# Layer 1's output projection: sums made by accumulating DMAs to DRAM, the last head's y taken from SBUF, and constants that fill a multiple of 64 bytes

## The chip, the cores and the metric

The kernel runs on one core of a Trainium2 chip. The metric is the device time of one execution in microseconds; the figure for a kernel is the median over runs. Beside it stands one profiled execution, with a trace of every instruction on the core's engines: PE (TensorE; PEld is its weight load), DVE (VectorE), ACT (ScalarE), POOL (GpSimd), and SP (SyncE, which here only issues loads).

## The reference

Two layers over 1,024 latent tokens and 256 context tokens, 1,024 channels. Layer 0 has 16 neighbourhood-attention heads and 4 bidirectional mLSTM heads; layer 1 has 16 bidirectional HGRN2 heads (gated linear attention). Each layer normalises its input, projects it, runs the heads, multiplies by a SiLU gate and projects back; the result goes through a learned gate and is added to the layer's input. The end of layer 1 is what the change is about:

```python
def merge(o, z):
    o = _rms(jnp.swapaxes(o, 1, 2).astype(z.dtype), h_norm.reshape(HG_HEADS, HG_VDIM))
    return (o.reshape(o.shape[:2] + (HG_VW,)) * jax.nn.silu(z)) @ w_out
...
x = x + gate * y_lat
```

Here y is 1,024 tokens by 2,048 (16 heads of 128), w_out is 2,048 by 1,024, and only latent tokens are returned. All of it is float32.

## The kernel before

**Exact products from pairs.** A float32 operand is split into a rounded high part and a low rest (`split`, L71: an ACT copy makes the high part, a DVE subtraction the rest). A product is three matmuls per slice of 128 (high x high, high x low, low x high: `dense`, L129 to L131, and `out_sum`, L858 to L860). So every operand costs one ACT and one DVE operation per 128x512 piece before PE may use it.

**Layer 1's heads.** For each of 16 heads, `hg_proj` projects forget gates and queries, `hg_intra` climbs seven levels (L1021 and L1051; a chain of small operations over PE, ACT and DVE), `hg_vz` projects values and gates (tiles wz), `hg_ctx` and `hg_scan` carry the state along. At the end of a head POOL scales y by its norm, and `hg_out` (L1150) transposes it in two halves of 512 tokens; ACT copies each half into the one buffer gyt (L1157) and POOL stores it in DRAM (`yd2`, L1158). While heads run, POOL also makes sums of blocks of w_out (`wo_sums`) and, for the first eight heads, the difference of y's two token halves (`y_diff`, stored in `sy`).

**Layer 1's output projection.** It is a product of 2x2 blocks in Winograd's form: y is cut into two halves of tokens and two of heads, w_out into four blocks of 1,024 x 512, and seven products of sums of blocks take the place of eight. Each product has four token tiles of 128, each tile 8 slices x 3 matmuls of 512 columns. The order is: first product (y's first tokens and heads; kept in `p`), seventh (`sy` with a sum of weights; added to `u`), second (first tokens, heads 8 to 15), then fifth, sixth, third and fourth. The first two and part of the second stand in the code as work that can fill PE while head 15 runs its chains. For the fifth, sixth and third the sums of y blocks are made as they are loaded: `sums` (L1426) loads one or two 128x512 tiles over SP and adds or subtracts on DVE (L1438) into `ysum` (tile oys). The sinks f2, f5, f6, f3 (from L1451 on) move results between `p`, `u` and `e`, with adds on POOL, and `final` (L1415) loads the residual tile from the scratch `x1`, adds, multiplies by the gate, adds the residual on POOL or DVE, and stores to the output from POOL's queue (L1423). Weights come over SP into a ring of raw buffers (woraw, 4) and are split into rings on the left (wo1) or the right side of SBUF (oy, w1).

**Order.** Instructions are put in each engine's order at build time by a planner that simulates a timeline from priorities; `urgent` moves work forward, `behind` puts one instruction behind another on its engine. On the chip each engine then runs its list in order and waits on semaphores. Loads go through SP's queue, stores and the sums' loads through POOL's.

**Places in SBUF.** Pools grow from the left and from the right; every tile starts at a multiple of 32 bytes. At the left stand the constants (from `ident` on), which take 1,632 bytes per partition from an address that is a multiple of 64, and behind them the left-hand pools of both layers. On the right stand the normalised input (hh, hl), layer 1's projection weights (w1), and the output projection's pool oy; they start at multiples of 64.

## Time and profile before

| | |
|---|---|
| median of 3 runs | 3446.57 us (3445.27 to 3448.31) |
| the profiled execution's own time | 3444.31 us |
| its span in the trace | 3442.5 us |
| PE busy | 3368.1 us, 98% of the span |
| DVE busy | 2051.4 us, 60% |
| ACT busy | 1407.0 us, 41% |
| POOL busy | 664.0 us, 19% |
| moved by DMA | 333.56 MB |
| mean granted PE clock | 0.992 |

Busy time is what the trace shows an engine at work. Matmuls overlap in it: one of 512 columns shows 0.39 us though the next starts 0.23 us later, so the pace is read from starts. A kernel whose PE is busy for 98% of the time can gain in two ways: at places where PE waits (here mostly at the start and in the last 220 us), or through matmuls that follow each other faster. A wait that is not on the way to the last instruction costs nothing.

### The profile page before, as it was taken

The numbers are of one execution on the slowest core, as the hardware profiler recorded it, in microseconds if no ns is written. First come the engines' busy times: TensorE is split into PE (matmuls) and PEld (weight loads), VectorE is DVE, ScalarE is ACT, GpSimd is POOL, SyncE is SP. The second block draws the span as 40 slices with busy tenths as digits, with TensorE's granted clock in tenths as the row PEclk, the third lists the DMA queues.
The fourth block names the chain that finished last, engine by engine and source line by source line (L and its number), as shares of the span: only waits on it lengthen the run. The fifth ranks groups of instructions, "written<-read, shape, count | busy, mean of one in ns | idle before, by whom it ended". The sixth has DMA issues, their size and how long they took to land.

```text
span 3442.5 us, 64358 instructions
## 1 busy us (share of the span) xinstructions
PE 3368.1 (98%) x25044; PEld 2972.1 (86%) x25044; DVE 2051.4 (60%) x4786; ACT 1407.0 (41%) x3310; POOL 664.0 (19%) x1036
## 2 busy tenths in 40 slices
PE   7999999999999999999999999999999999999988
PEld 5689999888989888898888999989999988889866
DVE  5336666566655466777666555555555555555657
ACT  5235544455444444454354333333333333333432
POOL 2121222122211111221100111111111111121023
PEclk9999999999999999999999999999999999999999
DMA  6522222232233443444652111111111111111364
GB/s 242 214 75 70 79 77 74 76 90 83 68 90 99 144 125 121 127 132 144 218 166 71 50 58 55 58 59 58 57 59 59 50 50 50 54 59 37 119 204 151
DMA packets 327152, 333.56 MB, mean 97 GB/s; under 512 B 30696, under 2 KB 277672, under 8 KB 324800
## 3 DMA queue, kind: packets, MB, share of 16 engines
q1 hardware_dynamic: 287808, 222.76, 21.8%
q0 software_dynamic: 39040, 106.69, 8.8%
q8 instruction: 197, 3.23, 0.4%
q14 instruction: 107, 0.88, 0.1%
HBM read 259.40 MB, written 69.79 MB: 96 GB/s over the span
## 4 chain that ended last, share of the span: by engine, by line
PE 87%; DMA 4%; issue 3%; DVE 3%; ACT 1%; POOL 1%; SPq 0%; POOLq 0%; DVEq 0%; ACTq 0%
PE mm L129 19%; PE mm L131 19%; PE mm L130 19%; PE s L1021 4%; PE acc L798 2%; PE tr L778 2%; PE mm L858 2%; PE mm L859 2%; PE mm L860 2%; PE s L579 2%; PE acc L570 2%; PE acc L560 1%; PE acc L1097 1%; PE tr L1033 1%; PE acc L1098 1%
## 5 line engine op out<-in xcount | busy, mean ns | idle before, releaser
L131 PE MATMUL mm<-hh,wl 128*128 128x512 f32 (+1 forms) x1600 | 584.2, 365 | 0.0
L129 PE MATMUL mm<-hh,wh 128*128 128x512 f32 (+1 forms) x1600 | 584.1, 365 | 0.0
L130 PE MATMUL mm<-hl,wh 128*128 128x512 f32 (+1 forms) x1600 | 583.6, 365 | 0.0
L129 PE MATMUL mm<-wh,hh 128*128 128x256 f32 (+1 forms) x1520 | 473.6, 312 | 1.7 <-ACT ev L314 1.0
L131 PE MATMUL mm<-wh,hl 128*128 128x256 f32 (+1 forms) x1520 | 470.1, 310 | 0.3 <-DVE hl L273 0.3
L130 PE MATMUL mm<-wl,hh 128*128 128x256 f32 (+1 forms) x1520 | 470.3, 309 | 0.0
L131 PEld LDWEIGHTS mm<-hh,wl 128*128 128x128 f32 x1600 | 301.6, 189 | 46.0 <-issue 0.3
L129 PEld LDWEIGHTS mm<-hh,wh 128*128 128x128 f32 x1600 | 301.9, 189 | 45.3 <-issue 0.8
L130 PEld LDWEIGHTS mm<-hl,wh 128*128 128x128 f32 x1600 | 301.8, 189 | 43.4 <-issue 0.2
L129 PEld LDWEIGHTS mm<-wh,hh 128*128 128x128 f32 x1520 | 286.3, 188 | 22.7 <-ACT ev L295 4.2
L131 PEld LDWEIGHTS mm<-wh,hl 128*128 128x128 f32 x1520 | 286.2, 188 | 13.5 <-issue 1.4
L130 PEld LDWEIGHTS mm<-wl,hh 128*128 128x128 f32 x1520 | 286.8, 189 | 12.5 <-issue 1.2
L129 PE MATMUL mm<-wzh,hh 128*128 128x256 f32 x1024 | 296.1, 289 | 0.6 <-ACT gEc L945 0.6
L131 PE MATMUL mm<-wzh,hl 128*128 128x256 f32 x1024 | 291.3, 284 | 0.0
L130 PE MATMUL mm<-wzl,hh 128*128 128x256 f32 x1024 | 290.5, 284 | 0.0
L74 DVE TENSOR_TENSOR wl<-wraw,wh 128x512 fp32r<-128x512 f32 x240 | 167.0, 700 | 175.4 <-ACT wh L73 172.1
L73 ACT CAST wh<-wraw 128x512 fp32r<-128x512 f32 x240 | 147.5, 619 | 243.4 <-PE mm L130 166.2
L129 PEld LDWEIGHTS mm<-wzh,hh 128*128 128x128 f32 x1024 | 193.5, 189 | 2.9 <-ACT gEc L945 0.8
L130 PEld LDWEIGHTS mm<-wzl,hh 128*128 128x128 f32 x1024 | 193.4, 189 | 1.7
L131 PEld LDWEIGHTS mm<-wzh,hl 128*128 128x128 f32 x1024 | 193.2, 189 | 1.2
L858 PE MATMUL mm<-woh,yh 128*128 128x512 f32 x422 | 169.8, 403 | 17.8 <-DVE og L1387 10.1
L1051 ACT COPY gksel<-gK 128x1024 f32<-128x1024 f32 x96 | 111.2, 1158 | 174.4 <-PE s L1021 128.9
(382 smaller groups left out, 7359.4 us busy)
## 6 DMA issues: line engine op xcount, KB each, us to landing
wraw<-in_wab_dram SPq DMA_DIRECT2D x112, 256.0 KB
wraw<-in_wc_dram SPq DMA_DIRECT2D x96, 256.0 KB
wraw<-yd SPq DMA_DIRECT2D x94, 256.0 KB
wraw<-in_wc_dram SPq DMA_DIRECT2D x128, 128.0 KB
md<-ev POOLq DMA_DIRECT2D x60, 256.0 KB, 2.7
mloz<-md SPq DMA_DIRECT2D x40, 256.0 KB
adar<-in_wada_dram SPq DMA_DIRECT2D x8, 1024.0 KB
adar<-in_wada_dram POOLq DMA_DIRECT2D x8, 1024.0 KB, 8.8
```

The costliest lines, as they stand in the source:

```text
L73: nc.scalar.copy(hi, x)
L74: nc.vector.tensor_tensor(out=lo, in0=x, in1=hi.bitcast(F32), op=ALU.subtract)
L129: mm(ps, lhsT=lh(k), rhs=rh(k), start=(start and k == 0), stop=False)
L130: mm(ps, lhsT=lh(k), rhs=rl(k), start=False, stop=False)
L131: m = mm(ps, lhsT=ll(k), rhs=rh(k), start=False, stop=(stop and k == nk - 1))
L570: nc.tensor.matmul(num, lhsT=qc[:, j, :], rhs=C[d][:, j, :], start=False, stop=(j == 1))
L579: nc.tensor.matmul(u, lhsT=st["k"][c][:, j * P : (j + 1) * P], rhs=vw, start=True, stop=True)
L778: nc.tensor.transpose(pt[:nk, i, :], pr[:, o : o + nk], self.ident)
L798: m = nc.tensor.matmul(yp[h64], lhsT=v[:, h64], rhs=pTs[hd][:nk, i, :], start=(i == turn[0]), stop=(i == turn[-1]), tile_position=(0, hd * ...
L858: mm(ps, lhsT=yh[k], rhs=w.h(kk), start=(kk == 0), stop=False)
L1021: self.nc.tensor.matmul(out[s], lhsT=lhsT, rhs=rhs, start=True, stop=True, tile_position=(0, b * 64))
L1051: nc.scalar.copy(ksel.rearrange("p (b s i) -> p b s i", s=2, i=h), pick(K))
```

## The change

- `y_diff` now stores second half less first half (the sign is turned) into three scratch arrays, `sy`, `s3` and `s6`, not into one.
- `hg_out` also stores the second half of heads 0 to 7 into `s5`. For heads 8 to 15 it adds to those arrays with accumulating DMAs: the first half (now negated) to `s3`, the second half to `s5`, `s6` and `s3`. So the y sums for the fifth, sixth and third products lie ready in DRAM, and `sums` is gone.
- The last head's first half is split from the SBUF copy (`near`, tiles lasth and lastl) and used for the second product's last slice, for all four token tiles; the second product's other seven slices run ahead of it. Two tiles of the fifth product's first four slices run ahead too, for which two more result banks are opened.
- Layer 0 stores its latent result straight into the output tensor; at the end `final` no longer loads a residual: it accumulates gate x sum into the output by DMA. The remaining adds of `p`, `u` and `e` go from POOL to DVE, and signs are turned to match.
- The first product's first y tiles are split into a free tile of the heads, its first four weight pieces into a ring that is free earlier, and later y splits are put behind the last head's level 5 (`late`). The raw ring of weights has 3 buffers, not 4; the y raw ring of that pool has 2, not 3.
- Constants: `hnc` holds its negative too (128 bytes, not 64), and `qknp` is a column of `qkn`.

```diff
     def y_diff(self, h, pool):
...
-        nc.gpsimd.tensor_tensor(out=x, in0=x, in1=z, op=ALU.subtract)
-        nc.gpsimd.dma_start(out=self.sy[h], in_=x)
+        nc.gpsimd.tensor_tensor(out=x, in0=z, in1=x, op=ALU.subtract)
+        for dst in (self.sy, self.s3, self.s6):
+            nc.gpsimd.dma_start(out=dst[h], in_=x)
...
-    def hg_out(self, h, yn, pool, y):
+    def hg_out(self, h, yn, pool, y, near=None):
...
-            yt = self.t(pool, [P, 512], F32, "gyt", 1)
-            nc.scalar.activation(yt, pt.rearrange("p a b -> p (a b)"), AF.Copy, scale=self.hnc[:, h : h + 1])
+            yt = self.t(*((near[2], [P, 512], F32, "lasty", 1) if near else (pool, [P, 512], F32, "gyt", 1)))
+            sign = 1 if h >= 8 and c == 0 else 0
+            nc.scalar.activation(yt, pt.rearrange("p a b -> p (a b)"), AF.Copy, scale=self.hnc[:, sign, h : h + 1])
             nc.gpsimd.dma_start(out=y[h, :, c * P : (c + 4) * P], in_=yt)
+            if h < 8 and c:
+                nc.gpsimd.dma_start(out=self.s5[h], in_=yt)
+            if h >= 8:
+                for dst in (self.s5, self.s6, self.s3) if c else (self.s3,):
+                    nc.gpsimd.dma_start(out=dst[h - 8], in_=yt, accum_op=ALU.add)
+            if near and c == 0:
+                self.split(near[0], near[1], yt)
...
-            self.hnc = load("hnc", [P, 16])
-            qkn = load("qkn", [P, 2])
-            self.qkn = self.t(cp, [P, 1], F32, "qknp")
+            self.hnc = self.t(cp, [P, 2, 16], F32, "hnc")
+            nc.gpsimd.dma_start(out=self.hnc[:, 0, :], in_=a["hnc"])
...
+            qkn = self.t(cp, [P, 3], F32, "qkn")
+            nc.gpsimd.dma_start(out=qkn[:, 0:2], in_=a["qkn"])
+            self.qkn = qkn[:, 2:3]
...
-                w = block(W[0:D, 0:512], wo * 8, None, [self.rawp, 3, "wraw"])
-                self.out_part(w, 0, 0, y2, yp, lambda t, ps: nc.scalar.copy(acc[0][:, t, :], ps))
-                w = block(self.sw[1], wr * 4 + wo * 4)
-                self.out_part(w, 0, 0, S, yp, lambda t, ps: add(u[:, t, :], ps, p[:, t, :]))
-                w2 = block(W[D : 2 * D, 0:512], wo * 4 + wr * 4)
...
+                w = block(W[0:D, 0:512], wr * 4 + wo * 4, None, [pool, 3, "wraw"])
+                ps = self.ps("mm", [P, 512])
+                self.out_sum(ps, w, 0, (0,), None, yp, 2, {0: ys})
+                nc.scalar.copy(p[:, 0, :], ps)
+                self.out_part(w, 0, 0, y2, yp, lambda t, ps: nc.scalar.copy(p[:, t, :], ps), None, range(1, 4), late=self.level)
+                w = block(self.sw[1], wo * 4 + wr * 4)
+                self.out_part(w, 0, 0, S, yp, lambda t, ps: add(u[:, t, :], p[:, t, :], ps, ALU.subtract))
+                w2 = block(W[D : 2 * D, 0:512], wo * 8)
+                m2 = []
+                for t in range(4):
+                    if t == 2:
+                        banks.close()
+                        es.enter_context(self.pp.phase(c=4))
+                    m2.append(self.ps("c" if t > 1 else "mm", [P, 512]))
+                    hi, lo = self.out_y(t, 1, y2, yp, 4, ks=((0, 4), (4, 3)))
+                    self.dense(m2[t], lambda i: hi[i], lambda i: lo[i], w2.h, w2.l, 7, True, False)
...
-                def final(tt, b, x, y, eng=nc.vector):
+                def final(tt, b, x, y, op_=ALU.add):
                     r, c = slice(tt * P, (tt + 1) * P), slice(b * 512, (b + 1) * 512)
-                    xt = self.t(op, [P, 512], F32, "oxh", 3)
-                    dma(out=xt, in_=self.x1[r, c])
-                    g = self.t(op, [P, 512], F32, "og", 2)
-                    add(g, x, y)
-                    nc.vector.tensor_tensor(out=g, in0=g, in1=gates[b], op=ALU.mult)
-                    add(xt, xt, g, eng)
-                    nc.gpsimd.dma_start(out=a["out"][r, c], in_=xt)
+                    g = self.t(op, [P, 512], F32, "og", 4)
+                    add(g, x, y, op_)
+                    add(g, g, gates[b], ALU.mult)
+                    nc.gpsimd.dma_start(out=a["out"][r, c], in_=g, accum_op=ALU.add)
...
                 def f5(t, ps):
                     nc.scalar.copy(e[:, t, :], ps)
-                    add(p[:, t, :], p[:, t, :], e[:, t, :], nc.gpsimd)
-                    add(e[:, t, :], u[:, t, :], e[:, t, :], nc.gpsimd)
+                    add(p[:, t, :], ps, p[:, t, :])
                     loads()
 
                 def f6(t, ps):
-                    s6 = self.t(op, [P, 512], F32, "os", 2)
-                    nc.scalar.copy(s6, ps)
-                    final(4 + t, 1, ps, e[:, t, :], nc.gpsimd)
-                    add(p[:, t, :], s6, p[:, t, :], nc.gpsimd)
-                    add(u[:, t, :], s6, u[:, t, :], nc.gpsimd)
+                    add(u[:, t, :], ps, u[:, t, :])
+                    add(p[:, t, :], ps, p[:, t, :])
+                    final(4 + t, 1, u[:, t, :], e[:, t, :])
                     loads()
...
-                self.out_part(w5, 0, 0, sums((0, 4), (8, 4, ALU.add, False)), yp, f5)
-                self.out_part(w6, 0, 0, sums(None, (0, 0, ALU.subtract, False)), yp, f6)
-                self.out_part(w3, 0, 0, sums(None, (8, 0, ALU.subtract, True)), yp, f3)
+                m5 += [self.ps("mm", [P, 512]) for _ in range(2)]
+                for t in range(2, 4):
+                    m5_part(t, 0, raws)
+                for t in range(4):
+                    m5_part(t, 4, raws)
+                    f5(t, m5[t])
+                self.out_part(w6, 0, 0, self.s6, yp, f6, raws)
+                self.out_part(w3, 0, 0, self.s3, yp, f3, raws)
                 self.out_part(w4, 4, 1, y2, yp, lambda t, ps: final(4 + t, 0, ps, u[:, t, :]), raws)
```

More of the change, by code (lines that the diff above doesn't have):

```diff
@@ L101, in piece @@
                 c = s.shape[1]
[L102 removed]
+                self.last_dma = nc.sync.dma_start(
                     out=r3[:, :, off : off + c],
@@ L1368, in build @@
                         st = self.hg_proj(h + 1, pool)
-                    self.hg_out(h, hv["A"], pool, self.yd2)
+                    if h == 15:
+                        rh.close()
+                        yp = es.enter_context(tc.tile_pool(name="oy", bufs=1, side="right"))
+                        last = [self.t(yp, [P, 512], F32R, t, 1) for t in ("lasth", "lastl")] + [yp]
+                    self.hg_out(h, hv["A"], pool, self.yd2, last)
                     for i in [h] if h < 12 else [2 * h - 12, 2 * h - 11] if h < 14 else []:
@@ L1373, in build @@
                         self.y_diff(h - 1, pool)
[L1375 to L1377 removed]
+                self.yraws = 2
+                wo, wr, raw = [(yp, "wo", 8)], [(self.wp, "w", 4)], [yp, 3, "woraw"]
                 assert self.slabs == 4
@@ new lines, in build @@
+                ys = ([], [])
+                for i, k in enumerate((0, 4)):
+                    raw8 = self.t(pool, [P, 512], F32, "wraw", 3)
+                    dma(
+                        out=raw8.rearrange("p (j t) -> p j t", j=4),
+                        in_=y2[k : k + 4, :, 0:P].rearrange("j p t -> p j t"),
+                    )
+                    self.split(near[:, 2 * i, :], near[:, 2 * i + 1, :], raw8)
+                    for part, n in zip(ys, (2 * i, 2 * i + 1)):
+                        part += [near[:, n, j * P : (j + 1) * P] for j in range(4)]
```

128 lines of the change are left out of this document (66 added, 62 removed).

## The prediction

> **What bounds the kernel now.** I read the table of windows over the end of the kernel first, because the output projection is where the diff works. Columns: stretch, its length, then busy time and count of PE, PEld, DVE, ACT and POOL, the granted clock, the DMA share and GB/s.
>
> ```profile
> core 0: us, PE busy (x) PEld busy (x) DVE busy (x) ACT busy (x) POOL busy (x), PEclk, DMA share, GB/s
> 3222.00:3250.00 28.00, 23.02 (x214) 18.02 (x213) 23.53 (x37) 17.23 (x30) 0.00 (x0) 0.88 0.65 208
> 3250.00:3299.20 49.20, 49.20 (x262) 41.59 (x260) 23.48 (x45) 18.68 (x41) 3.10 (x4) 1.00 0.38 118
> 3299.20:3313.00 13.80, 8.12 (x29) 5.93 (x28) 5.60 (x9) 6.12 (x16) 2.88 (x4) 0.88 0.44 134
> 3313.00:3391.00 78.00, 65.12 (x249) 49.73 (x250) 66.93 (x81) 29.56 (x53) 36.33 (x29) 0.90 0.82 248
> 3391.00:3434.70 43.70, 43.66 (x184) 34.68 (x182) 28.36 (x42) 11.43 (x19) 14.52 (x15) 0.98 0.50 165
> 3434.70:3442.50 7.80, 0.00 (x0) 0.00 (x0) 2.07 (x3) 0.00 (x0) 0.54 (x1) 0.65 0.09 34
> ```
>
> PE is busy throughout the second and the fifth stretch. In the first, third and fourth it is idle for 5.0, 5.7 and 12.9 us, and what it does run there goes at a granted clock of 0.88, 0.88 and 0.90, which costs about another 2.8 (0.12 x 23), 1.0 and 6.5 us. So the tail loses 7.8 + 6.7 + 19.4 = 33.9 us to waiting. The same table in thirds of the fourth stretch, and the waits (total, times, longest), say for what:
>
> ```profile
> 3313.00:3340.00 27.00, 25.24 (x100) 19.84 (x101) 21.05 (x31) 10.44 (x19) 8.83 (x9) 0.94 1.04 311
> 3340.00:3365.00 25.00, 22.12 (x85) 16.57 (x85) 19.88 (x25) 10.78 (x20) 13.46 (x10) 0.93 0.96 292
> 3365.00:3391.00 26.00, 17.76 (x66) 13.32 (x66) 26.00 (x27) 8.35 (x15) 14.05 (x12) 0.84 0.46 141
> ```
>
> ```profile
> PE mm L858 <- DVE og L1387: 10.1, 3, 7.0
> ...
> ACT woh L73 <- DMA woraw<-sw: 23.4, 8, 9.2
> ACT yh L73 <- DVE oys L1438: 21.0, 12, 4.5
> ...
> PE mm L858 <- ACT yh L73: 3.5, 2, 1.9
> ```
>
> The first two thirds are bound by DMA (share 1.04 and 0.96; ACT waits 23.4 us for weights), the last by DVE, which is busy for all 26.00 us. The last wait row is from the first stretch: the first product lacks its split y while head 15 climbs its levels.
>
> Outside the tail PE is the bound without a gap, so there only the pace of its matmuls counts. That pace is not one number. Timeline rows (start, duration, engine, line), first and last of runs without a break:
>
> ```profile
> 1656.12 0.39 PE L858 MATMUL mm<-woh,yh 128*128 128x512 f32 x1
> ...
> 1686.11 0.39 PE L858 MATMUL mm<-woh,yh 128*128 128x512 f32 x1
> ```
>
> ```profile
> 3404.16 0.40 PE L860 MATMUL mm<-woh,yl 128*128 128x512 f32 x1
> ...
> 3434.27 0.39 PE L860 MATMUL mm<-woh,yl 128*128 128x512 f32 x1
> ```
>
> ```profile
> 191.34 0.40 PE L129 MATMUL mm<-hh,wh 128*128 128x512 f32 x1
> ...
> 201.89 0.40 PE L129 MATMUL mm<-hh,wh 128*128 128x512 f32 x1
> ```
>
> ```profile
> 1656.00:1686.00 30.00, 30.00 (x134) 1.00 0.98 303
> 3404.00:3434.00 30.00, 30.00 (x130) 1.00 0.44 140
> ```
>
> Between the starts lie 132, 129 and 45 matmuls: 227.2, 233.4 and 234.4 ns each. The two windows (PE busy and count, clock, DMA) show it by count, 134 against 130 in 30 us, both at clock 1.00. The first two runs are the same kind of matmul on the same kind of tile. What differs is where the operands lie: in the first run both are in the right-hand pool, in the others the moving one and the stationary one are on different sides. The program places every tile on a multiple of 32 bytes. The constants before it take 1,632 bytes, so every left-hand pool of weights starts 32 past a multiple of 64; the right-hand tiles start on multiples of 64.
>
> **The change part by part.**
>
> *Constants.* hnc grows from 64 to 128 bytes, and qkn takes in qknp (32 less): 1,632 becomes 1,664 = 26 x 64, and everything on the left moves by 32 bytes. Left against right then agrees modulo 64, as in the 227.2 ns run. The counts (group rows: count | busy us, mean ns; one of three lines each, the other two have the same count; first three from before 1654 us, the fourth from 3313 us on, the last from 1860 to 3222):
>
> ```profile
> L129 PE MATMUL mm<-hh,wh 128*128 128x512 f32 x384 | 152.6, 397 | 0.0
> ...
> L129 PE MATMUL mm<-wh,hh 128*128 128x512 f32 x240 | 100.3, 419 | 0.2 <-ACT wh L73 0.2
> ...
> L129 PE MATMUL mm<-wxh,hh 128*128 128x512 f32 x80 | 32.6, 410 | 0.5 <-ACT wxh L73 0.5
> ```
>
> ```profile
> L858 PE MATMUL mm<-woh,yh 128*128 128x512 f32 x136 | 56.6, 416 | 12.5 <-DVE og L1387 10.1 <-ACT yh L73 2.2
> ```
>
> ```profile
> L130 PE MATMUL mm<-wzl,hh 128*128 128x256 f32 x1018 | 288.8, 284 | 0.0
> ```
>
> Of the 136 some 128 read the left-hand ring (four products x 4 tiles x 8). 3 x (384 + 240 + 80 + 128) = 2,496 matmuls x 6.3 ns = 15.7 us; I take 15 saved, since gaps too small to see may swallow some. For 256 columns it is less clear:
>
> ```profile
> 1984.16 0.28 PE L130 MATMUL mm<-wzl,hh 128*128 128x256 f32 x1
> ...
> 1987.55 0.28 PE L129 MATMUL mm<-wzh,hh 128*128 128x256 f32 x1
> ```
>
> ```profile
> 2428.76 0.28 PE L129 MATMUL mm<-hh,wh 128*128 128x256 f32 x1
> ...
> 2431.26 0.28 PE L129 MATMUL mm<-hh,wh 128*128 128x256 f32 x1
> ```
>
> The first run (29 matmuls, 116.9 ns) has its operands on different sides, the second (21, 119.0 ns) on the same side: here agreement is slower by 2.1 ns. The wz matmuls number 3 x 1018 and some, so 6.4 us are to be lost if they go to 119.0, nothing if not. I take 4. The other 256-column products, in layer 0, I take as unchanged.
>
> By the Trainium skill (TensorE: Matmul & The Clock Gate, Part 2: What happens when you issue a matmul), PE reads weights and moving data through two independent ports, so that loading weights takes nothing from the running matmul. By that rule the shift does nothing and this term is 0, not -11; the two runs of 227.2 and 233.4 ns speak against it, unless something other than the addresses sets them apart.
>
> *The sums leave DVE and POOL.* These are group rows of DVE from 3313 to 3434.7, and the last from 3250 to 3299, where POOL is nearly idle (3.10 us):
>
> ```profile
> L74 DVE TENSOR_TENSOR wol<-woraw,woh 128x512 fp32r<-128x512 f32 x32 | 27.2, 874 | 4.4 <-ACT woh L73 4.4
> ...
> L1438 DVE TENSOR_TENSOR oys<-oys,oyz 128x512 f32<-128x512 f32 x16 | 13.8, 874 | 3.9 <-DMA oyz<-yd 2.4 <-DMA yraw<-yd 1.3
> ...
> L1438 DVE TENSOR_TENSOR oys<-oyz,oys 128x512 f32<-128x512 f32 x8 | 11.0, 1390 | 0.0
> ...
> L1387 DVE TENSOR_TENSOR oxh<-oxh,og 128x512 f32<-128x512 f32 x3 | 2.1, 692 | 0.1
> ```
>
> ```profile
> L74 DVE TENSOR_TENSOR wol<-woraw,woh 128x512 fp32r<-128x512 f32 x8 | 5.3, 690 | 2.5 <-ACT woh L73 2.5
> ```
>
> DVE loses the y sums (24.8 us) and the residual's adds (2.1), gains 12 adds from POOL (12 x 0.69 = 8.3), and its 32 weight splits go from 874 back to 690 ns without POOL beside them (-5.9). 66.93 + 28.36 = 95.3 us becomes 71 over about 100 us of matmuls: no longer the bound. Loads: of the 40 y tiles, 16 residual tiles and 32 weight pieces of the last four products, 256 KB each, the fifth product's 8 second operands and the 16 residual tiles are no longer loaded; the accumulating stores add a read each, but on the other queue. So both bounds give way. What is late next is the sixth product, whose sink has four DVE operations per tile: with two y splits and two weight splits 8 x 0.69 = 5.5 us, against 24 matmuls x 0.2272 = 5.45 us. I take 14 of the 19.4 us (bounds 6, if the weight ring, now 3 raw buffers instead of 4, keeps ACT waiting, and 19).
>
> *The last head's y from SBUF.* The second product runs seven of eight slices without head 15, then the fifth product's first four for two tiles: 84 + 24 matmuls against 24 before, 19 us more, that may run before head 15's result is there. That covers the 6.7 us of the third stretch: I take 5 (0 to 6.7). In the first stretch four weight pieces and the first y are split early into tiles that are already free: 3 of 7.8 us (0 to 6); the split copies queued behind level 5 keep ACT free for the chain.
>
> *In the heads.* Heads 0 to 7 issue three more stores, heads 8 to 15 four accumulating ones, 0.62 us of POOL each (row below). POOL idles before most of them. The place that can hurt is the single yt buffer: ACT's second copy waits until the first half's DMAs, now with an accumulation on s3, have read it. Head 11's wait has room:
>
> ```profile
> 2935.44 0.69 ACT L1157 ACTIVATE gyt<-tr,hnc 128x512 f32<-128x512 f32 x1 [4.87 <-PE tr L1155]
> ...
> 2944.49 0.69 ACT L1157 ACTIVATE gyt<-tr,hnc 128x512 f32<-128x512 f32 x1 [1.90 <-PE tr L1155]
> ```
>
> ```profile
> 2936.42 0.61 POOL L1158 DMA_DIRECT2D yd<-gyt  x1 [3.33 <-ACT gyt L1157]
> ...
> DMA to landing us min/median/max: 2.4/2.4/4.2
> ```
>
> The accumulation is issued by 2937.7 and has 6.8 us until ACT wants the buffer. The trace has no accumulating DMA. Its nearest row is the plain store, 2.4 us; a read and a write one after the other would be 4.8. Either fits. ACT's queue behind it holds the copy of v and the next level's ksel, for which PE would wait. I take 2 us over all heads (0 to 10).
>
> *The end.* After the last matmul one of the residual's adds goes (0.69, the oxh row above), and the last store becomes an accumulation: between 2.4 and 4.8 us instead of 2.4, I take +1.2. Sum +0.5 (-0.7 to +2).
>
> **Sum.** -15 + 4 - 14 - 5 - 3 + 2 + 0.5 = -30.5 us on the profiled execution's own 3444.3: 3413.8. The median of the runs is 2.3 us above that execution: 3416.
>
> **The rivals.** (a) *The addresses do nothing*: the 6 ns have another cause. For it: one agreeing pair runs slower at 256 columns. Against: two different places at 233 to 234 ns. Without -15 and +4: 3427. This is where the rule of the Trainium skill above would lead. (b) *The tail finds a new bound*: three raw buffers and the order on SP's queue keep weights late, or the sixth product holds DVE. For it: 23.4 us of waits for weights. Against: 24 of 88 loads fewer. Only 6 + 2 + 1 of the 22 us come: 3429. (a) and (b) together: 3440. (c) *Accumulations are slow*, and the kernel gets slower. Place: ACT waiting at L1157 in heads 8 to 15, PE behind it. With a landing of L us each of eight heads loses L - 8.8 (6.8 of room, some 2 us that PE's two result banks cover), and the last store L - 2.4. This eats 32 us when 8(L - 8.8) + L - 2.4 = 32, at L = 11.6, about five plain stores; at 13 us it is 3416 + 44 - 2 = 3458. For it: nothing like it was measured, and two accumulations on s3 in one head must follow one another. By the Trainium skill (DMA: Bandwidth & Descriptors, Rules for kernel authors) an accumulation must wait for the earlier one's semaphore; the trace has none to show it. Against: one read more doesn't make five stores. (d) *Better*: all of the bounds come, 19 + 6.7 + 6 in the tail, 16 and no loss from the addresses: 3446.6 - 47 = 3399.
>
> **How the numbers follow.** Forecast 3416 (its own range 3406 to 3424): 0.45. (a) 0.13, (b) 0.16, both 0.04, (c) 0.10, (d) 0.12. Range 3398 to 3440: beyond it lie (c) and the edges of (d) and of both. This kernel's times tell apart about 0.2%, 6.9 us, so faster is below 3439.7: 0.45 + 0.13 + 0.16 + 0.12, less edges, 0.83; same 0.07; slower 0.10.
>
> **What would show it.** The 3313 to 3391 stretch with DMA share under 0.9, DVE under 80% and no wait for oys; 227 ns between 512-column matmuls at 191 us; wz at 119 ns; landing of s3 under 6.8 us; PE idle in the tail under 12 us in all. It is wrong if layer 0 ends at the same time as before, if ACT's wait at L1157 grows in heads 8 to 15, or if PE waits for weights in place of sums.

## The result and the profile after

| | before | changed |
|---|---|---|
| median, us (5 runs of each, side by side) | 3445.27 (3442.29 to 3448.31) | 3416.5 (3411.4 to 3420.42) |
| ratio | | 0.9917, 95% interval 0.9906 to 0.9929 |
| profiled execution: own time / span, us | 3444.31 / 3442.5 | 3411.4 / 3409.6 |
| mean granted clock | 0.992 | 0.994 |

The kernel is faster by 28.8 us at the medians, and the prediction was 3416. The profiled execution of the changed kernel lies at the low end of its five runs: between the two traces lie 32.9 us.

The windows of the changed kernel over the end of the program (stretch, length, busy time and count of PE, PEld, DVE, ACT, POOL, then clock, DMA share, GB/s):

```profile
core 0: us, PE busy (x) PEld busy (x) DVE busy (x) ACT busy (x) POOL busy (x), PEclk, DMA share, GB/s
3218.00:3246.00 28.00, 26.88 (x232) 22.03 (x233) 20.64 (x31) 16.03 (x29) 0.00 (x0) 1.00 0.53 161
3246.00:3290.80 44.80, 44.63 (x245) 38.09 (x243) 27.30 (x52) 21.03 (x45) 2.26 (x3) 1.00 0.58 176
3290.80:3320.20 29.40, 24.33 (x108) 19.47 (x107) 13.11 (x21) 9.65 (x23) 10.50 (x13) 1.00 0.72 179
3320.20:3399.10 78.90, 78.84 (x336) 63.87 (x336) 52.77 (x85) 30.91 (x53) 9.39 (x11) 0.98 0.78 194
3399.10:3409.60 10.50, 0.00 (x0) 0.00 (x0) 1.36 (x2) 0.00 (x0) 0.85 (x1) 0.66 0.17 25
```

From 3320 on (the second half of the fifth product, then the sixth, third and fourth) PE now runs without a gap: it is idle for 0.06 us until 3399. DVE is busy for 67% of that time, where it had been busy for all of the last third before, and DMA for 78%, where it had been at 104% and 96% in the first two thirds. The first stretch has lost its idle time too (28.00 - 26.88 = 1.1 us against 5.0), and its clock is 1.00 instead of 0.88. What is left stands in the third stretch, 5.1 us, and in the fifth, where no matmul runs for 10.5 us; before, that end was 7.8.

To see where the 32.9 us come from, one follows the same piece of work through both traces. Rows of the changed kernel: the first matmul of the long run in layer 0's output (before: 1656.12), a copy of head 11's y (before: 2935.44), and the copy of the last half of the last head's y.

```profile
1651.31 0.39 PE L861 MATMUL mm<-woh,yh 128*128 128x512 f32 x1
```

```profile
2931.67 0.69 ACT L1164 ACTIVATE gyt<-tr,hnc 128x512 f32<-128x512 f32 x1 [4.85 <-PE tr L1161]
...
3301.18 0.69 ACT L1164 ACTIVATE lasty<-tr,hnc 128x512 f32<-128x512 f32 x1 [1.63 <-PE tr L1161]
```

The last of them in the kernel before:

```profile
3308.92 0.69 ACT L1157 ACTIVATE gyt<-tr,hnc 128x512 f32<-128x512 f32 x1
```

| from ... to | before, us | changed, us | gain, us | the prediction's terms there |
|---|---|---|---|---|
| start, layer 0's output | 1656.12 | 1651.31 | 4.8 | 13 (constants) |
| to head 11 | 1279.32 | 1280.36 | -1.0 | -4 (wz), -2 (heads) |
| to the last head's y | 373.48 | 369.51 | 4.0 | 3 (first stretch) |
| to the end of the last matmul | 125.74 | 97.86 | 27.9 | 5 + 14 + 2 (constants) |
| to the end of the span | 7.84 | 10.56 | -2.7 | -0.5 |

The last matmul ends at 3434.66 before and at 3399.04 after. The sum of the forecast came out right, and its terms did not: layer 0 gave a third of what it was to give, the tail gave a third more, and the end took five times its price.

Each row compares two single traces. Six kernels that are alike up to head 11 (the changed one and runs 6, 7, 9, 10 and 11) reach the place in layer 0's output between 1650 and 1655 us and head 11's copy between 2930 and 2936. So the gains of the first two rows hold only to some 3 us either way; the 27.9 of the tail is far outside such scatter.

### The profile page after: what moved, and what is told of

Same layout as the page of the kernel before. It is cut to its first block, busy times and chain, and to the rows that moved or that the text cites. A ratio compares the mean times of both kernels' runs of the same rounds, so it can differ in the third digit from the quotient of the medians.

```text
span 3409.6 us, 64360 instructions
## 1 busy us (share of the span) xinstructions
PE 3353.0 (98%) x25044; PEld 2967.1 (87%) x25044; DVE 2019.0 (59%) x4772; ACT 1401.5 (41%) x3307; POOL 666.3 (20%) x1064
## 4 chain that ended last, share of the span: by engine, by line
PE 88%; issue 4%; DMA 3%; DVE 2%; POOL 1%; ACT 1%; SPq 0%; POOLq 0%; DVEq 0%; ACTq 0%
PE mm L130 19%; PE mm L132 19%; PE mm L131 19%; PE s L1024 4%; PE acc L799 2%; PE tr L779 2%; PE mm L861 2%; PE mm L863 2%; PE mm L862 2%; PE acc L571 2%; PE s L580 2%; PE acc L561 1%; PE acc L1102 1%; PE tr L1036 1%; PE acc L1103 1%
## 5 line engine op out<-in xcount | busy, mean ns | idle before, releaser
L1071 DVE TENSOR_TENSOR gQ<-gQ,gF 128x1024 f32<-128x1024 f32 x112 | 139.2, 1243 | 54.1 <-PE s L1024 53.4
```

Source lines behind the costliest of these rows:

```text
L1071: nc.vector.tensor_tensor(out=v, in0=v, in1=tot, op=ALU.mult)
```

## The experiments

Every kernel ran on one chip with runs of the kernel before beside it, and every ratio below is to those runs, as the 0.9917 is. A difference in us between two kernels is taken from their ratios where nothing else is said, since the medians of the kernel before go from 3443.7 to 3445.6 us there. Differences of about 5 us between two such kernels are at the edge of what the runs tell apart, so where one stage is meant, the time between two events of the same trace is given too.

### 1 and 2: 32 bytes in each kernel

```diff
+            nc.vector.memset(self.t(cp, [P, 8], F32, "pad"), 0.0)
             edge = es.enter_context(tc.tile_pool(name="edge", bufs=1, side="right"))
```

> The kernel before with 32 unused bytes put behind the constants, nothing else: every left-hand tile moves by 32 bytes, as the change moves it. Theory A (from the paces in the trace of the changed kernel: matmuls of 512 columns cost 227 to 228 ns where the two operands lie a multiple of 256 bytes apart, 229 at 64 bytes from one, 232.5 at 128, 233.5 at 32 or 96; wz products get 0.8 ns slower, the other left-against-right products of 256 columns 0.9 ns faster): -1.6 -1.1 -1.7 +2.5 -3.0 -0.9 = about -6 us, 3439.5 against 3445.3 for the kernel before, ratio 0.998. The prediction's step (all 2,496 matmuls go to 227.2 ns, wz to 119.0): -11 us, ratio 0.997. Rival (a), the addresses do nothing: ratio 1.000.

> The changed kernel with 32 unused bytes behind the constants: the left-hand tiles go back to 32 past a multiple of 64, the rest of the change stays. Theory A: +6 us on the changed kernel's 3416.5, so 3422.5, ratio to the kernel before 0.9933. The prediction's step: +11, 3427.5, ratio 0.9948. Rival (a): 3416.5, 0.9917. In the trace the matmuls of layer 0 with 512 columns go from 232.5 back to 233.5-234 ns, those of the tail that take the left-hand ring from 229 to 233 ns.

Measured: the kernel before with the padding 3437.99 us, ratio 0.9981 (0.9972 to 0.9989, 11 runs), 6.5 us faster; the changed kernel with it 3424.04, ratio 0.9933 (0.9921 to 0.9946), 5.5 us slower than without. The addresses are worth about 6 us, both ways round. The expectation of 11 lies outside the first interval (9.6 at most), and 0 lies outside it too. The second run by itself settles less, since its interval overlaps that of the changed kernel.

### 3: 128 bytes more

The same line with 32 elements in place of 8, in the changed kernel.

> The changed kernel with 128 unused bytes behind the constants. Agreement modulo 64 stays as it is; the distance between left-hand and right-hand operands changes by 128 modulo 256: in layer 0 from 128 to 0. Theory A (the distance modulo 256 sets the pace): 2,112 matmuls of 512 columns in layer 0 go from 232.5 to about 227.5 ns, -10; wz products (distance 64 to the other side) between 0 and -7; layer 0's products of 256 columns +2: in all -8 to -15, 3401 to 3408, ratio 0.987 to 0.989. Rival (only modulo 64 counts, as the prediction had it): 3416.5, ratio 0.9917, and 232.5 ns stays.

Measured: 3403.72 us, ratio 0.9875 (0.9861 to 0.9888). Another 14.5 us faster than the changed kernel (12.8 at the medians), for 128 bytes that nothing uses. Rows of the timeline, first and last matmul of an unbroken run of 46 in layer 0, at the same place of the program as the run at 191 us in the prediction; changed kernel first, then the one with the padding:

```profile
189.89 0.39 PE L130 MATMUL mm<-hh,wh 128*128 128x512 f32 x1
...
200.39 0.39 PE L130 MATMUL mm<-hh,wh 128*128 128x512 f32 x1
```

```profile
191.07 0.40 PE L130 MATMUL mm<-hh,wh 128*128 128x512 f32 x1
...
201.29 0.39 PE L130 MATMUL mm<-hh,wh 128*128 128x512 f32 x1
```

45 intervals: 233.3 ns, hardly less than the 234.4 of before, and then 227.2 ns. So agreement modulo 64 was not the condition. The tail moves the other way in the same kernel; its last 321 to 326 intervals, changed kernel, then with 128 bytes:

```profile
3324.00 0.41 PE L130 MATMUL c<-woh,yh 128*128 128x512 f32 x1
...
3398.65 0.39 PE L863 MATMUL mm<-woh,yl 128*128 128x512 f32 x1
```

```profile
3316.65 0.41 PE L132 MATMUL c<-woh,yl 128*128 128x512 f32 x1
...
3391.55 0.40 PE L863 MATMUL mm<-woh,yl 128*128 128x512 f32 x1
```

229.0 ns over 326 intervals against 233.4 over 321. Windows of 74 us inside these two runs say that it isn't the clock, which is 1.00 in both:

```profile
3324.00:3398.00 74.00, 74.00 (x325) 60.64 (x324) 49.51 (x79) 28.59 (x49) 9.39 (x11) 1.00 0.77 192
```

```profile
3317.00:3391.00 74.00, 74.00 (x319) 59.63 (x318) 48.96 (x78) 28.16 (x48) 9.39 (x11) 1.00 0.76 179
```

Theory A holds. Taking each matmul's two tile addresses from the built program and the mean time to the next matmul of the same kind from the trace, one gets this (distance: address of the moving minus that of the stationary operand, modulo 256; all operands are 4 bytes an element):

```
columns  operands, place    before      changed     +32 bytes   +128 bytes
512      h,w   layer 0     160: 234.0   128: 232.6   96: 233.4    0: 228.4
512      wo,y  tail         32: 232.0    64: 228.8   96: 231.7  192: 231.8
256      wz,h  heads        32: 116.8    64: 117.6   96: 119.8  192: 114.7
256      w,h   layer 0      96: 119.6   128: 118.8  160: 118.2    0: 119.5
512      h,w   heads         0: 228.9     0: 228.5    0: 228.2    0: 228.0
```

The last row is the control: both operands lie on the same side there, so no padding moves them against each other, and it stays within 0.9 ns. With 512 columns a distance of 0 is the fastest; with 256 it is among the slowest, and 192 the fastest. That 0 and 128 differ rules out a period of 64 or 128 bytes; whether the period is 256 or a multiple of it was not tried apart.

### 4: distances chosen from that table

```diff
+            off = right.enter_context(tc.tile_pool(name="off", bufs=1, side="right"))
+            nc.vector.memset(self.t(off, [P, 16], F32, "off"), 0.0)
             self.open_h(right)
...
             lk = self.fp = l1.enter_context(tc.tile_pool(name="hgk", bufs=1))
+            nc.vector.memset(self.t(lk, [P, 32], F32, "off1"), 0.0)
...
+                nc.vector.memset(self.t(op, [P, 48], F32, "off2", 1), 0.0)
                 wl1 = wl.enter_context(tc.tile_pool(name="wo1", bufs=1))
```

> The changed kernel with three paddings and nothing else: 64 unused bytes under layer 0's right-hand operands, 128 under the left-hand tiles of layer 1's heads, 192 under the left-hand tiles of the tail. Theory A (the distance moving minus stationary operand, modulo 256, sets the pace, with the paces of the runs above: 256 columns 114.65 ns at 192, 117.6 at 64, 118.8 at 128; 512 columns 229 at 64, 231.8 at 192, 232.6 at 128, 227.2 at 0): layer 0's moving weights go from distance 128 to 192 (3,300 matmuls of 256 columns, -13.7 us; 960 of 512 columns, -0.6), its moving hh from 128 to 64 (1,152 x 3.6 = -4.1), wz from 64 to 192 (-9), the tail from 64 to 0 (-0.9): -28 us, 3388 (3384 to 3394), ratio 0.984. Rival (256 columns at 192 are fast only for wz, by its kind and not its place): -14 us, 3402, ratio 0.988.

Measured: 3394.49 us, ratio 0.9858 (0.9843 to 0.9873): the fastest of all, 22 us below the changed kernel at the medians (20 by the ratios) and 51 (49) below the kernel before. It lies between the theory (3388) and the rival (3402), and the paces say that the rival is wrong: layer 0's products of 256 columns, no wz among them, went from 118.8 to 115.5 ns in the mean. The longest unbroken run of them, first and last row, in the changed kernel and then here:

```profile
1121.53 0.27 PE L130 MATMUL mm<-wh,hh 128*128 128x256 f32 x1
...
1132.56 0.28 PE L130 MATMUL mm<-wh,hh 128*128 128x256 f32 x1
```

```profile
1109.48 0.28 PE L130 MATMUL mm<-wh,hh 128*128 128x256 f32 x1
...
1120.03 0.28 PE L130 MATMUL mm<-wh,hh 128*128 128x256 f32 x1
```

93 intervals: 118.6 and 113.4 ns. In the tail the distance is 0 now, and the pace is a little under the 228 that the table has for it, 321 intervals of 226.7 ns:

```profile
3307.40 0.40 PE L132 MATMUL c<-woh,yl 128*128 128x512 f32 x1
...
3380.17 0.39 PE L863 MATMUL mm<-woh,yl 128*128 128x512 f32 x1
```

Most of the 6 us that are missing of the 28 lie in layer 0: its moving weights of 256 columns stayed at 115.5 in the mean, not 114.65, and those of 512 got no faster (233.2 ns at 192 against 232.5).

### 5 to 7: the sums, the residual, POOL's additions, one at a time

Run 5 gives SP and DVE the sums for s6 and s3 again, in the tail; run 6 loads the residual and adds it on DVE; run 7 puts 12 additions back on POOL (the first diff below doesn't show the loader of the sums and what the heads no longer store, the last one not the four additions of the fifth product):

```diff
...
-                self.out_part(w6, 0, 0, self.s6, yp, f6, raws)
-                self.out_part(w3, 0, 0, self.s3, yp, f3, raws)
+                self.out_part(w6, 0, 0, sums(True, 0, ALU.subtract), yp, f6)
+                self.out_part(w3, 0, 0, sums(False, 8, ALU.add), yp, f3)
```

```diff
...
+                    xt = self.t(op, [P, 512], F32, "oxh", 3)
+                    dma(out=xt, in_=a["out"][r, c])
...
-                    nc.gpsimd.dma_start(out=a["out"][r, c], in_=g, accum_op=ALU.add)
+                    add(xt, xt, g)
+                    nc.gpsimd.dma_start(out=a["out"][r, c], in_=xt)
```

```diff
...
-                    add(u[:, t, :], ps, u[:, t, :])
-                    add(p[:, t, :], ps, p[:, t, :])
+                    s6 = self.t(op, [P, 512], F32, "os", 2)
+                    nc.scalar.copy(s6, ps)
+                    nc.gpsimd.tensor_tensor(out=u[:, t, :], in0=s6, in1=u[:, t, :], op=ALU.add)
+                    nc.gpsimd.tensor_tensor(out=p[:, t, :], in0=s6, in1=p[:, t, :], op=ALU.add)
```

> The changed kernel, but the y sums of the sixth and the third-weight product (s6, s3) are made in the tail again: SP loads both operands, DVE adds (16 additions), and the heads issue no accumulations onto s3 and s6 and no copies to them. s5 stays as it is. The count of 256 KB loads in the last four products is then the old one. Theory (DVE bound per product): in the sixth product each tile has 10 DVE operations of 0.69 us, 6.9 us against 5.45 us of matmuls, so 4 x 1.45 = +6 us there, less 0 to 2 us saved in the heads: 3420 (3418 to 3424), with DVE over 80% busy between 3320 and 3400. Rival 1 (DVE has room, 52.8 of 78.9 us, and only the adds on POOL had slowed it): 3416.5. Rival 2 (accumulations in the heads cost something there): the heads end over 2 us earlier.

> The changed kernel, but the residual is loaded by SP into SBUF, added by DVE and the tile stored plainly, as before the change (16 loads of 256 KB more, 16 DVE operations of 0.69 us more, no accumulations into out). Theory: 11 us more on DVE still fit (64 of 79 us), and the end after the last matmul falls from 10.6 to about 8 us: -1 (-3 to +2), 3415.5. The prediction's step (both bounds come back in part): +3 to +5 in the tail.

> The changed kernel with the additions of the sinks of the fifth and sixth product back on POOL (12 additions; ACT copies the sixth product out of PSUM for them again). Theory: POOL beside DVE takes DVE's 32 weight splits from 690 back towards 870 ns, but DVE loses the 12 additions (8.3 us): 0 to +2, 3417.5. Rival (the adds on POOL were what held the tail): over +4, 3421.

Measured: 3416.94, 3416.63 and 3417.24 us, ratios 0.9920 (0.9906 to 0.9934), 0.9921 (0.9907 to 0.9935) and 0.9922 (0.9909 to 0.9936): none can be told from the changed kernel by the time. In the traces the way from the last head's y to the end of the last matmul is 103.5, 102.5 and 102.3 us instead of 97.9, so each costs 4 to 6 us there, by one trace of each; in six kernels whose tail differs from the changed one in nothing but distances or the last store (the changed kernel and runs 2, 3, 4, 10 and 11) it lies between 97.8 and 100.6. By that measure the sums come out as expected, the residual as the prediction's step had it and not as the theory (-1) did, and POOL's additions at the theory's upper end or its rival's lower (2 to 4). The times are too close to decide any of the three.

The three do not cost at the same place. PE's longest wait behind the last head's y that the changed kernel doesn't have, in runs 5 and 6:

```profile
PE mm L861 <- DVE oacc L1412: 3.4, 1, 3.4
PE mm L130 <- ACT yh L73: 6.1, 1, 6.1
```

With the sums back, PE waits for a late addition of DVE's in a sink. With the residual back, PE waits for DVE no longer than 0.9 us; the 6.1 us are a wait at 3317.8 for ACT's split of the fifth product's y. ACT had waited there 8.3 us at a time for a weight piece, on a queue of SP's that now carries the residual tiles too; in the changed kernel its longest such wait there is 1.4 us, and PE's gap of 3.5 us at 3320 does not come on top in run 6. In run 7 PE has two waits of 1.4 and 1.1 us for splits of ACT's, and DVE's weight splits are slower:

```profile
L74 DVE TENSOR_TENSOR wol<-woraw,woh 128x512 fp32r<-128x512 f32 x22 | 16.6, 773 | 9.0 <-ACT woh L73 8.9
```

POOL is busy there for 26.6 us of 83. In run 5, with the sums on DVE but POOL at 9 us, the same 22 splits take 688 ns as in the changed kernel: it is POOL's work beside them, not DVE's load, that lengthens them.

### 8: all three together

The three diffs above in one kernel. What is left of the change in the tail is s5, the order of the products and the last head's y from SBUF.

> The changed kernel with the three edits of the runs above put back together: s6 and s3 summed in the tail, the residual loaded and added by DVE, the 12 additions on POOL. What stays of the change in the tail is the last head's y from SBUF, the order of the second and fifth product, and s5. Alone each of the three cost 0 to 1 us. Theory (each bound had room for one of them, not for all; together DVE gets 16 x 0.69 + 16 x 0.69 = 22 us more, slower beside POOL, and DMA 6 MB more): DVE is over 90% busy in the last 80 us and PE waits, +10 to +18 us, 3430. Rival (the gain of the tail is all in the order of the products and the last head's y, the sums are worth nothing): 3416 to 3419.

Measured: 3420.1 us, ratio 0.9928 (0.9916 to 0.9941): 4 us slower by the runs, which is between rival and theory; the two intervals overlap, so the runs leave room for some 10 us and for none. The trace is clearer: the way to the last matmul is 109.8 us instead of 97.9, 11.9 more. The window of the same products as above (from the fifth's second half on):

```profile
3321.10:3410.30 89.20, 82.83 (x334) 65.58 (x334) 71.29 (x100) 32.41 (x56) 29.45 (x24) 0.94 0.68 218
```

Its groups of DVE there, instructions | busy us, mean ns | idle before:

```profile
L74 DVE TENSOR_TENSOR wol<-woraw,woh 128x512 fp32r<-128x512 f32 x22 | 16.6, 763 | 2.0 <-ACT woh L73 2.0
L1412 DVE TENSOR_TENSOR oys<-oys,yraw 128x512 f32<-128x512 f32 x16 | 12.9, 820 | 0.0
```

And its waits in that window (total, times, longest):

```profile
PEld mm L862 <- DVE wol L74: 5.3, 3, 3.1
PE mm L862 <- DVE wol L74: 4.0, 3, 2.7
```

PE is idle for 6.4 of the 89 us, at a clock of 0.94, and waits most for DVE's weight splits, which take 763 ns beside a busy POOL (29 us); in the changed kernel, with POOL at 9 us, the same 22 take 688:

```profile
L74 DVE TENSOR_TENSOR wol<-woraw,woh 128x512 fp32r<-128x512 f32 x22 | 14.9, 688 | 12.7 <-ACT woh L73 12.5
```

DVE is busy for 80% of the window and DMA for 68%, neither of them all the time: my "over 90%" was wrong, and the wait is for single operations that come late. So the two bounds of the kernel before, DMA at 104% and DVE at 100%, are not back in this kernel.

### 9: the last head's y from DRAM

```diff
-                    hi, lo = self.out_y(t, 1, y2, yp, 4, ks=((0, 4), (4, 3)))
-                    self.dense(m2[t], lambda i: hi[i], lambda i: lo[i], w2.h, w2.l, 7, True, False)
+                    hi, lo = self.out_y(t, 1, y2, yp, 4, ks=((0, 4), (4, 4)))
+                    self.dense(m2[t], lambda i: hi[i], lambda i: lo[i], w2.h, w2.l, 8, True, True)
...
-                for t in range(4):
-                    at = slice(t * P, (t + 1) * P)
...
```

> The changed kernel, but the second product takes all eight slices from DRAM, the last head's too, tile by tile (the split copies of the last head's y in SBUF are made and not used). Theory: PE waits from the first tile's eighth slice until head 15's result has gone to DRAM and back, some 6.5 us after 3301, and the 84 + 24 matmuls that covered it come after: +6 (4 to 9), 3422.5, with the new gap on the second product's y; the gap of 3.5 us at 3316.6 goes, because it is covered by these matmuls. The prediction's step: +5. Rival (order doesn't matter, since DMA is behind anyway): 0 to +1.

Measured: 3427.46 us, ratio 0.9951 (0.9939 to 0.9964), 11.7 us slower: more than the 9 that the range allowed. The waits of PE from 3246 to 3320 in this kernel:

```profile
PE tr L1161 <- POOL gA L1123: 4.9, 1, 4.9
PE c L130 <- ACT yh L73: 4.2, 1, 4.2
PE mm L130 <- ACT yh L73: 2.1, 1, 2.1
PE acc L1102 <- DVE gA L1122: 2.0, 1, 2.0
```

The two rows with yh are the expected wait, 6.3 us in all, both in the second product: the 2.1 ahead of the first tile's second half, the 4.2 ahead of the third tile's (at 3313.5). The fifth product's gap does go, as expected: its second half begins at 3336.2 without a wait. The other two rows, 6.9 us, were not expected: without the 84 + 24 matmuls ahead of it, PE has nothing to do while the last head's own chain (gA on DVE and POOL) ends. So the cover served two waits. This is not a step back to the kernel before, which ran the first half of the second product's first two tiles (24 matmuls) ahead; in this trace it is 12 matmuls.

### 10 and 11: the last store

Run 10 folds the residual of the last tile into u early and stores that tile plainly from POOL; run 11 does the same and issues that store from SP:

```diff
+                add(u[:, 3, :], u[:, 3, :], gates[0], ALU.mult)
+                add(u[:, 3, :], u[:, 3, :], xl)
...
+                    add(g, ps, gates[0], ALU.mult)
+                    add(g, g, u[:, 3, :])
+                    nc.gpsimd.dma_start(out=a["out"][r7], in_=g)
```

> The changed kernel, but the last of the 16 output tiles has its residual (and the u term) folded in early, in SBUF, so that after the last matmul come a multiplication, an addition and a plain store, not an accumulating one. Theory: the 10.56 us from the end of the last matmul to the end of the span go to about 7.2 (before: 7.84 with three DVE operations), so -3.4 us, 3413. The prediction's step put the accumulation at 1.2 us: then -1.2, 3415.3. Rival: the end is set by the accumulations of the three tiles ahead, which are not changed: 0.

> As the run with the plain last store, but that last store is issued by SP and not by POOL. Theory: in the trace of the changed kernel the end is set by POOL's last DRAIN, which lasts until 7.2 us after the issue of its last DMA (4.1 before the change, 6.0 with a plain last store), while the data has landed some 4 us earlier. With the last store on SP, POOL's last DMA is issued 5.5 us earlier and its drain runs beside the last tile: from the end of the last matmul to the end of the span 5 to 6 us instead of 10.6 (9.1 with the plain store on POOL), so -5 us, 3411.5. Rival (the drain waits for the end of the program whoever stores last): 9 us stay.

Measured: 3411.61 us, ratio 0.9898 (0.9883 to 0.9914), and 3408.96, ratio 0.9897 (0.9884 to 0.9911): both intervals overlap that of the changed kernel, so the stretch behind the last matmul is what tells. From the end of the last matmul to the end of the span it is 9.1 and 5.3 us, against 10.56 in the changed kernel and 7.84 before. Only the 5.3 is as expected. The rows of POOL's sequencer at the program's last line (duration ns min/median/max, first and last start), for the kernel before, the changed one, and runs 10 and 11, say why:

```profile
L1621 POOLq DRAIN  x3: 46/98/4642, 3437.1 to 3442.3; - x3
```

```profile
L1668 POOLq DRAIN  x3: 46/93/8072, 3400.8 to 3409.3; - x3
```

```profile
L1682 POOLq DRAIN  x3: 46/102/6633, 3403.0 to 3410.2; - x3
```

```profile
L1682 POOLq DRAIN  x3: 46/93/8270, 3402.0 to 3410.7; - x3
```

The longest of the three drains starts with POOL's last store and holds the end until it is done: 3437.1 + 4.6 = 3441.7 before, 3400.8 + 8.1 = 3408.9 after. In run 11 it is as long as ever, but it starts at 3402.0, before DVE's last two operations, and most of it lies beside the last tile. Not all: it ends at 3402.0 + 8.3 = 3410.3, about 1 us behind SP's wait for its own store (3409.2), and so still ends last, 0.7 us ahead of the end of the span. SP's store goes out right behind the last operation of DVE:

```profile
3406.49 0.69 DVE L1413 TENSOR_TENSOR og<-og,oacc 128x512 f32<-128x512 f32 x1
3407.21 0.35 SPq L1536 DMA_DIRECT2D out_dram<-og  x1
```

What sets the drain's length shows in part in the other runs. It is 4.6 us in the kernel before, without accumulating DMAs; 6.1 in run 8, with accumulations onto s5 alone; 6.6 in runs 6 and 10, with all those in the heads and a plain last store; 6.7 in run 5, with those onto s5 and onto the output; and 8.1 to 8.4 in the changed kernel and the rest. So it is longer with accumulations in the heads, long before the end, and longer again when POOL's last DMA is one.

The Trainium skill (VectorE: DVE Perf Modes, The DRAIN you can't avoid) gives about 12 ns for drains that the runtime puts ahead of and behind a program, on every engine. The ones above stand at the program's own last line, and POOL's longest takes 4,642 to 8,270 ns, so that figure does not price them.

### 12: all of it, and the fifth product in another order

The paddings of run 4, the last store of run 11, and the fifth product's last slice moved behind the others:

```diff
                 for t in range(4):
-                    m5_part(t, 4, raws)
+                    m5_part(t, 4, raws, 3)
+                for t in range(4):
+                    m5_part(t, 7, raws, 1)
                     f5(t, m5[t])
```

> The changed kernel with the three paddings, the last store on SP, and the fifth product's last slice (k = 7, the one that waits for head 15's accumulation onto s5) taken after the other slices of all four tiles, by loads of its own. Theory: -28, -5, and up to -3.5 from the gap at 3316.6, of which I take -2: 3381 (3376 to 3388), ratio 0.982.

Measured: 3397.64 us, ratio 0.9864 (0.9850 to 0.9877): no better than run 4 with the paddings alone. The end is 5.3 us as in run 11, but the way from the last head's y to the last matmul is 106.9 us instead of 97.8. Its waits from 3300 to 3325:

```profile
PE mm L130 <- ACT yh L73: 4.4, 3, 3.1
PEld mm L861 <- DVE oacc L1416: 3.9, 1, 3.9
PE mm L861 <- DVE oacc L1416: 3.3, 1, 3.3
```

The new order is a loss of 9 us: the four sinks of the fifth product now come in one burst behind its last slice, and the sixth product waits for DVE's additions in them (3.3 us), beside three waits for y. With smaller ones PE's waits come to 8.9 us there, against one of 3.3 in run 4, and the granted clock is 0.89 in the 38.7 us behind the last head's y, where run 4 has 0.97 in the first 18.6 us and 0.96 after them. Run 4 with run 11's store and without this order, some 3389 by the sum of the two, was not run.

## Why the prediction was right, and where it was not

*Right in the sum, by errors that cancel.* 3416 against 3416.5 is luck in part. By the table of the result, layer 0 gave 8 us less than its term, the stretch to head 11 lost 5 less, the tail gave 7 more, and the end cost 2 more.

*Constants (-15 and +4): the step that failed in its reason.* It said that left against right "agrees modulo 64, as in the 227.2 ns run", and sent 2,496 matmuls to 227.2 ns. Two runs of rows could not tell "modulo 64" from "modulo 256", and the tiles of the 227.2 ns run were apart by a multiple of 256. The change moved layer 0 from distances of 160 and 96 to 128 and the tail from 32 to 64: 1 to 1.4 ns and 3.2 ns for each matmul instead of 6.3. The wz products lost 0.8 ns and not 2.1 (2.5 us in all, not 4), and the other products of 256 columns in layer 0, taken as unchanged, gained 0.9. Together 6 us instead of 11 (runs 1 and 2). At the place the prediction named, 191 us, the pace is 233.3 and not 227.

*Rival (a), the addresses do nothing,* is wrong by runs 1 to 4. By the Trainium skill (TensorE: Matmul & The Clock Gate, Part 2: What happens when you issue a matmul) weights and moving data come through two independent ports, from which the prediction drew that the shift does nothing; here a matmul's pace of 226.7 to 233.4 ns at a clock of 1.00 depends on where its two operands lie against each other.

*The sums leave DVE and POOL (-14).* Three of the edits put back together cost 11.9 us on the way to the last matmul; the sums for s5 were not put back, so 14 fits, and no run shows it whole. The prediction had two bounds, DMA and then DVE, both full; both are gone in the changed kernel. But what the three edits cost comes without either bound being full again (0.68 and 80% in run 8): as waits for single operations of DVE (runs 5 and 8) and for loads that come later (run 6). That POOL beside them lengthens DVE's splits was right (773 ns in run 7, 763 in run 8, against 688). The feared next bound, the sixth product's four operations, does not show: PE has no gap behind 3320, and rival (b) falls with it.

*The last head's y (-5 and -3).* Without the cover of 84 + 24 matmuls 11.7 us are lost (run 9), more than the 5 taken, because it covers the last head's own chain too; but run 9 has less cover than the kernel before, so 11.7 is too much for this term. Of the tail's 27.9 us, run 8 explains 11.9 and runs 1 and 2 some 2 to 3 by the addresses; the other 13 are the order, the last head's y and s5 together, which no run takes apart. The first stretch gave its 3: PE idles there for 1.1 us instead of 5.0. But the third stretch is not free of waits. Of PE's waits from 3218 to 3400 these are the three longest:

```profile
PE c L130 <- ACT yh L73: 3.5, 1, 3.5
PE mm L130 <- ACT lasth L73: 1.3, 1, 1.3
PE mm L861 <- ACT woh L73: 1.1, 1, 1.1
```

The 3.5 us are new: the fifth product's second half needs the last head's y out of s5. SP's own waits from 3300 to 3322 show what it stands behind:

```profile
SPq L842 <- DMA s<-lasty: 4.0, 1, 4.0
```

SP holds its whole queue for 4.0 us until an accumulation of the last head's y has landed. A part of what the new order gained is given back to an accumulation one product later.

*Heads (+2) and rival (c).* Accumulations onto s3, s5 and s6, from issue to landing (min, median, max), first of heads 8 to 15, then of heads 8 to 14 alone, and what ACT waited for at the copy into gyt:

```profile
DMA to landing us min/median/max: 3.8/5.2/10.4
...
DMA to landing us min/median/max: 3.8/4.7/6.8
```

```profile
  PE tr L1161: 70.4, 21
  DMA s<-gyt: 3.7, 1
```

The price was for the accumulation onto s3 that must have read the buffer before ACT's second copy. In heads 8 to 14 that one lands within 3.8 to 4.3 us, inside the bounds of 2.4 and 4.8. Those behind another accumulation take up to 6.8, and the last head's, with SP's loads beside them, up to 10.4. Rival (c) decides from 11.6 on, and even the longest is below that. Only one head made ACT wait, for 3.7 us. From layer 0's output to head 11 the trace is 1.0 us longer, with the wz products' loss in it.

*The end (+0.5).* The step that failed: it priced the last store's landing, and the end hangs on POOL's drain behind it: +2.7. The term had the wrong mechanism, not only a wrong size.

## What to carry to other kernels

Where PE is the bound without a gap, compare the start-to-start time of the same kind of matmul at several places and look at the distance of its two operands in SBUF; some unused bytes between two pools were worth 20 to 22 us here, two thirds or more of what the change gave. Undo the parts of a change together as well as one at a time: three edits that each cost 4 to 6 us in one trace's tail when taken back, and nothing that the times could tell, cost 12 there and 4 in the times together. And see what ends last behind the last matmul: a last store on another queue than POOL's hid most of POOL's drain here.

## What the runs showed of the hardware

- The pace of matmuls with 4-byte operands depends, in windows with a granted clock of 1.00 too, on the distance of the moving from the stationary operand; taken modulo 256 it goes from 226.7 to 234 ns with 512 columns and from 113.4 to 120 ns with 256, and the best distance differs (0 and 192). Why is open: which reads meet was not measured, and classes with the same distance still spread by 1 to 2 ns.
- An accumulating store of 256 KB from POOL takes 0.85 us to issue at the end against 0.54 of a plain one, and 1.08 us in the median in the heads against 0.62. In the heads it lands in 3.8 to 4.3 us where no other accumulation is ahead of it and in up to 6.8 behind another, against 2.4 of the plain store there.
- POOL's long drain at the program's end takes 4.6 us in the kernel before, 8.1 in the changed one, 6.6 with a plain last store (run 10) and 6.1 where accumulations go onto s5 alone (run 8). It ends last in all of these and in run 11, where it began 3.8 us ahead of the end of the last matmul. What in the accumulations lengthens it was not measured.
